# A transformer layer on one core: row maxima as a stream of their own, w_out scaled within its split, another order in the first chunk

## The chip, the cores and the metric

The kernel runs on one core of one Trainium2 chip. The metric is the device time of one execution in microseconds, from the kernel's start to its end. The core has a matmul engine (PE, with PEld for its weight loads), a vector engine (DVE), an activation engine (ACT), a general engine (POOL) and an engine that issues transfers (SP); each works through its own list of instructions in order, and they wait for one another by semaphores.

## What is computed

One layer over 2,048 positions of width 1,024 in float32:

```
xn = rms_norm(x, mix_norm_g);  h = xn @ w_in
q, k, v, f_logit, z = split(h)                  # 8 heads of 64; z is 2 x 512
c = cumsum(log_sigmoid(f_logit + b_f))
s[t, u] = q_t . k_u / 8 + c[t] - c[u],  u <= t
attn = softmax(s) @ v
zu, zv = split(gelu(z));  zv = layer_norm(zv)
sgu = zu * (w_s (masked, 128 x 128 per group) @ zv + b_s)
merged = concat(rms_norm(attn), rms_norm(sgu))  # times out_norm_g
x = x + merged @ w_out
xn = rms_norm(x, ffn_norm_g);  gate, up = split(xn @ w_gate_up)
x = x + (silu(gate) * up) @ w_down
out = rms_norm(x, final_norm_g)
```

## The kernel before

Matmul operands are kept as two parts, a high one (`hi_of`, a rounding cast, on ACT) and the rest (`lo_of`, value minus high part, on DVE or POOL), and each product is three matmuls: high by high, high by low, low by high. The source emits instructions in an order that serves as priority; a scheduler then fixes each engine's list at build time by its own estimate of when operands are ready, so an engine's list need not follow the source. What a list holds is then kept to on the chip: an instruction that waits holds up all behind it.

**Projection (stage 1).** The positions go in four chunks of 512. For each, x is loaded transposed, scaled and split (`Chunk.halves`), the split is stored to memory as XS for later use (`Chunk.keep`, two stores of 512 KB for each of four parts), row squares of the untransposed x give the norm r1 (`Chunk.square`), and r1 is turned to a row by transposes on PE (`Chunk.row`, L270). Weights come in four pieces each through `weight` or `whole`: a load from POOL's queue into one of two raw buffers, a cast on ACT, a subtraction on DVE. In the first chunk v is projected first (`v_part`, into four PSUM banks of the tag "mm"); `v_close` scales and splits the four results (ACT L428, DVE L429), and the gate matmuls L482 take the first bank that comes free. Then come four groups of 24 matmuls for q and four for k (L509). After each group `between` advances three generators: the forget gates of this chunk (`forget_rows`: an ACT and DVE chain up to lf, then transposes and products on PE from L311 on, the result stored as AUG), the preparation of the next chunk (`Chunk.steps`) and the early row maxima.

**Row maxima.** The softmax needs the maximum of each query row over its keys. `one_max` is one matmul (L337, 128 queries by up to 512 keys, into one of two PSUM buffers) and one DVE reduction (L339, or with the causal mask L342). For a head h and a query chunk j there are 4(j+1). `max_split` and `max_rows` bring the result to memory (md), from where it joins the query tile A as two more rows. `early_max(j)` does heads 0 to 7 of chunks 0 and 1 and heads 0 to 4 of chunk 2 within stage 1, with query and key tiles (A, D) of its own. What is left, chunk 3 of all heads and chunk 2 of heads 5 to 7, is done in `prep`.

**Attention (stage 2).** The 32 units (h, j) run head by head; a unit has 4(j+1) steps, 320 in all. A step is `qk` (two matmuls L624 and L625, a mask L627 on the diagonal, exp on ACT L629, the split of the result, Ph on ACT and Pl on DVE) and, one step later, `pv_of` (L640 to L642). At a unit's first step `prep` is started for the unit two ahead (AHEAD): it loads keys, values and queries and, where the maxima are still missing, spreads them over this one unit's steps. Between the steps runs `gates`: the z projection (`z_proj`, L672, 256 k steps), GELU, norm and `z_mix`, spread by a count over the steps up to ZEND = 293. Before the loop starts, w_s is loaded, masked and split, and the norm's constants are loaded (L933 to L942). The split of w_u, z's first weight, stands at the end of stage 1.

**w_out.** From step 276 on, as soon as z's k steps are all issued, `out_weights` takes one slice of 128 x 512 a step, 16 in all: POOL multiplies it by out_norm_g (`gain`, L799), ACT casts it, POOL subtracts. At step 300 the output stage begins (`out_tiles`), then the FFN, whose matmuls L1296 fill the span from some 1,250 us on.

## Time and profile before

| | us |
|---|---|
| three runs | 2510.0, 2509.7, 2504.14 |
| median | 2509.7 |
| the profiled execution | 2512.58 |
| its span, first to last instruction | 2510.8 |
| PE busy in it | 2437.3 |

All rows below are from that one profiled execution; times in rows count from the start of its span. The profile says of each instruction when it ran, how long the engine had been idle before it, and what released it. A matmul's end is modelled, so the time from one start to the next says more than the duration.

### The profile page before, as it was taken

Reading aid. Unit: us, or ns where it says so; the run is one execution under the profiler, and the core shown is the slowest. Engines: PE = TensorE matmul, PEld = TensorE weight load, DVE = VectorE, ACT = ScalarE, POOL = GpSimd, SP = SyncE. Lnnn points to the kernel's source line nnn. Section 1 sums busy time; section 2 is a strip of 40 time slices with the busy share of each in tenths; the row PEclk is TensorE's granted clock in tenths of the full one; section 3 lists DMA queues with packets and bytes.
Section 4 is the critical chain, followed back from the end, with each engine's and each line's share of the span. In section 5 each row is a group of like instructions: output and inputs, shape, how many; then the busy total and the mean of one; then the engine's idle time right before and its main releaser. Section 6 shows DMA issues by size and latency. Waiting matters only on the chain. (4 is left out here: it accounts for less than half of the span.)

```text
span 2510.8 us, 31035 instructions
## 1 busy us (share of the span) xinstructions
PE 2437.3 (97%) x10857; PEld 1949.1 (78%) x10857; DVE 1562.2 (62%) x2537; ACT 1054.5 (42%) x1787; POOL 555.6 (22%) x442
## 2 busy tenths in 40 slices
PE   7899999999999989999999999999999999999998
PEld 5677777787777776877788888878888877888876
DVE  4457485555456666455755555775555587586887
ACT  4312236667777666333423333433232342232333
POOL 1000000000000024122223323233232234454441
PEclk9999999999999988999999999999999999999999
DMA  9766574334433336665422232342322335455454
GB/s 307 259 223 207 162 210 131 93 99 108 112 95 96 89 88 171 187 207 174 159 84 85 84 93 68 93 142 76 93 68 84 93 109 193 168 180 187 134 189 150
DMA packets 351646, 348.25 MB, mean 139 GB/s; under 512 B 54428, under 2 KB 275092, under 8 KB 350466
## 3 DMA queue, kind: packets, MB, share of 16 engines
q1 hardware_dynamic: 349186, 337.88, 43.5%
q0 software_dynamic: 2304, 8.39, 1.1%
q8 instruction: 86, 1.41, 0.2%
q14 instruction: 70, 0.57, 0.1%
HBM read 229.47 MB, written 116.72 MB: 138 GB/s over the span
## 5 line engine op out<-in xcount | busy, mean ns | idle before, releaser
L102 ACT CAST wh<-raw 128x512 fp32r<-128x512 f32 (+2 forms) x500 | 309.3, 624 | 803.0 <-PE pp L1296 648.3
L107 DVE TENSOR_TENSOR wl<-raw,wh 128x512 fp32r<-128x512 f32 (+2 forms) x500 | 371.6, 752 | 116.5 <-ACT wh L102 115.2
L107 DVE TENSOR_TENSOR Pl<-Pt,Ph 128x512 fp32r<-128x512 f32 (+1 forms) x320 | 201.3, 635 | 198.0 <-ACT Ph L102 190.2
L1027 POOL TENSOR_TENSOR raw<-raw 128x512 f32<-128x512 f32 (+1 forms) x124 | 166.3, 1342 | 542.3 <-DMA raw<-in_w_gu_dram 374.1
L629 ACT ACTIVATE Pt<-st 128x512 f32<-128x512 f32 (+1 forms) x320 | 168.4, 532 | 157.0 <-PE st L625 83.3
L672 PE MATMUL z<-wh,xz 128*128 128x512 f32 x512 | 201.6, 403 | 0.0
L102 ACT CAST Ph<-Pt 128x512 fp32r<-128x512 f32 (+1 forms) x320 | 176.2, 556 | 13.5 <-DVE Pl L107 2.4
L1027 DVE TENSOR_TENSOR raw<-raw,raw 128x512 f32<-128x512 f32 (+1 forms) x112 | 133.4, 1192 | 73.1 <-POOL raw L1027 69.2
L339 DVE TENSOR_REDUCE mx<-mx_ps 128x1 f32<-128x512 f32 x192 | 127.9, 685 | 29.2 <-PE mx_ps L337 28.1
L642 PE MATMUL pv<-Pl,V 128*128 128x512 f32 (+1 forms) x320 | 121.9, 381 | 11.2 <-DVE Pl L107 11.2
L337 PE MATMUL mx_ps<-D,A 72*128 72x512 f32 (+5 forms) x320 | 121.8, 402 | 11.3 <-DVE mx L339 5.9
L624 PE MATMUL st<-A,D 74*128 74x512 f32 (+1 forms) x320 | 121.5, 380 | 1.8 <-ACT Pt L629 1.7
L640 PE MATMUL pv<-Ph,V 128*128 128x512 f32 (+1 forms) x320 | 122.7, 383 | 0.4 <-ACT Ph L102 0.3
L625 PE MATMUL st<-B,C 128*128 128x512 f32 (+1 forms) x320 | 119.7, 374 | 0.0
L641 PE MATMUL pv<-Ph,V 128*64 128x512 f32 (+1 forms) x320 | 117.0, 366 | 0.0
L672 PEld LDWEIGHTS z<-wh,xz 128*128 128x128 f32 x512 | 96.7, 189 | 18.9
L1296 PE MATMUL pp<-R2h,wh 128*128 128x512 f32 x264 | 105.2, 398 | 4.9 <-ACT u L1085 4.9
L1296 PE MATMUL pp<-R3h,wl 128*128 128x512 f32 x264 | 104.3, 395 | 2.6 <-DVE wl L107 2.6
L1296 PE MATMUL pp<-R2h,wl 128*128 128x512 f32 x264 | 105.0, 398 | 0.2 <-DVE wl L107 0.2
L1296 PE MATMUL pp<-R1h,wl 128*128 128x512 f32 x264 | 104.4, 395 | 0.7 <-DVE wl L107 0.7
L1296 PE MATMUL pp<-R2l,wh 128*128 128x512 f32 x264 | 104.5, 396 | 0.0
L1296 PE MATMUL pp<-R5h,wh 128*128 128x512 f32 x264 | 104.4, 395 | 0.0
(338 smaller groups left out, 6203.0 us busy)
## 6 DMA issues: line engine op xcount, KB each, us to landing
raw<-in_w_gu_dram SPq DMA_DIRECT2D x88, 512.0 KB
HD<-hT SPq DMA_DIRECT2D x44, 512.0 KB
xz<-XS SPq DMA_DIRECT2D x32, 512.0 KB
XA<-xa SPq DMA_DIRECT2D x27, 512.0 KB
xa<-XA SPq DMA_DIRECT2D x24, 512.0 KB
raw<-HD SPq DMA_DIRECT2D x24, 512.0 KB
xb<-XA SPq DMA_DIRECT2D x24, 512.0 KB
XA<-xb SPq DMA_DIRECT2D x21, 512.0 KB
```

Of the source, the lines that this page charges most:

```text
L102: nc.scalar.copy(o, i)
L107: eng.tensor_tensor(o, i, f(h), ALU.subtract)
L337: nc.tensor.matmul(pm[:, 0:n], lhs, Dt[0 : lhs.shape[0], 0:n], start=True, stop=True)
L339: nc.vector.tensor_reduce(mx[:, a, s : s + 1], pm, AX.X, ALU.max)
L624: nc.tensor.matmul(st[:, off:], Dt[:, b * P : (b + 1) * P], A[:, off:], start=True, stop=False)
L625: nc.tensor.matmul(st[:, off:], C[:, b * P : (b + 1) * P], B[:, off:], start=False, stop=kb < 4 * j)
L629: nc.scalar.activation(Pt[:, off:], st[:, off:], AF.Exp)
L640: nc.tensor.matmul(pv[:, off:], V[:, 0:P], Ph[:, off:], start=kb == 0, stop=False)
L642: nc.tensor.matmul(pv[:, off:], V[:, 0:P], Pl[:, off:], start=False, stop=kb == 4 * j + 3)
L672: nc.tensor.matmul(pz, xz[:, a, k, :], w[b][:, k, :], start=n == 0, stop=n == 3 * KT - 1)
L1027: (nc.vector if e == "v" else nc.gpsimd).tensor_tensor(o, a, b, op)
L1296: nc.tensor.matmul(pm, a[:, k, :], b[:, k, :], start=on is None and k == 0 and e == 0, stop=k == it.kh - 1 and e == 2, skip_group_check=n ...
```

## The change

- `forget_rows` gives way three times in place of once before its transposes, for chunks 0 and 1.
- `early_max` becomes `max_stream`, which takes a list of units, pools and buffer counts. Stage 1 calls it for the same units as before. Stage 2 calls it once for all that are left, with two query and two key tiles of its own in a new pool, loaded one key tile ahead; it is advanced by a count, 166 turns over LEND = 276 steps with a lead of 12. `prep` has no maxima any more. `max_due` runs the stream on where a unit that starts within three steps still lacks them.
- w_q's pieces 2 and 3 are loaded and split after `v_close` rather than before the v projection.
- The XS stores of chunk 0 move from its own q groups to those of chunk 1.
- The split of w_u moves from the end of stage 1 into z's first six k steps; w_s and the constants of the norm (`z_consts`) are loaded at z's third k step and split at its thirteenth.
- In `out_weights` ACT scales by out_norm_g as it casts, and one DVE operation scales and subtracts; POOL's two operations go, and so does one empty step.

```diff
+LEND = 276
...
-        yield
+        for _ in range(3 if j < 2 else 1):
+            yield
...
-    def early_max(j):
-        jobs = [(h, s) for h in range(HE[j]) for s in range(j + 1)]
+    def max_stream(units, pl, ps, pp, nd, ahead):
+
+        jobs = [(h, j, s) for h, j in units for s in range(j + 1)]
...
                 if s == 0:
-                    A = As[h] = T(p1, [66, CH], F32R, "A")
+                    A = As[h, j] = T(pl, [66, CH], F32R, "A", bufs=2)
...
-                Dt = Ds[n] = T(p1, [66, CH], F32R, "D", bufs=ND)
+                Dt = Ds[n] = T(pl, [66, CH], F32R, "D", bufs=nd)
                 ldr(Dt[0:64], KH[pr][s][o : o + DH])
                 ldr(Dt[64:66].rearrange("r (b t) -> r b t", t=P), aug_rows(h, s, slice(2 * j, 2 * j + 2)))
-        late = None
-        PF = j + 1
-        for n in range(PF):
+        def turn():
+            max_rows(pp, T(ps, [P, 4, P], F32, "mx_ps" if ps is ps2_[0] else "tp", **kw), *late)
+        late, kw = None, {"bufs": NMX} if ps is ps2_[0] else {}
+        for n in range(ahead):
             get(n)
-        for n, (h, s) in enumerate(jobs):
-            get(n + PF)
+        for n, (h, j, s) in enumerate(jobs):
+            get(n + ahead)
             if s == 0:
-                mx = T(p1, [P, 4, 4], F32, "mx")
+                mx = T(pp, [P, 4, 4], F32, "mx")
             for a in range(4):
-                one_max(ps1, p1, a, j, s, As[h][:, a * P : (a + 1) * P], Ds[n], mx)
+                one_max(ps, pp, a, j, s, As[h, j][:, a * P : (a + 1) * P], Ds[n], mx)
                 yield
                 if a == 2 and late is not None:
-                    max_rows(p1, T(ps1, [P, 4, P], F32, "tp"), *late)
+                    turn()
                     late = None
             if s == j:
-                late = (h, j, max_split(p1, j, mx))
-        yield
-        max_rows(p1, T(ps1, [P, 4, P], F32, "tp"), *late)
+                late = (h, j, max_split(pp, j, mx))
+        yield
+        turn()
...
-    wq = whole(wgt, w_in[:, 0:512], "w")
+    wq, get_q, halves_q = weight(wgt, w_in[:, 0:512], "w")
+    for i in range(2):
+        get_q(i)
+        halves_q(i)
     load_mats()
...
     nxt.row()
     for tt in range(4):
         v_close(pms[tt], nxt, tt)
+    for i in range(2, 4):
+        get_q(i)
+        halves_q(i)
     wk = whole(wgt, w_in[:, 512:1024], "w")
...
+                if c == 1 and which == 0:
+                    first.keep(pr)
                 qh = T(p1, [P, CH], F32R, "qh")
                 ql = T(p1, [P, CH], F32R, "ql")
                 if c == 0:
-                    if which == 0:
-                        xc.keep(pr)
...
-        early = early_max(c) if c < NCH - 1 else iter(())
-    for i in range(4):
-        if i > 1:
-            get_u(i)
-        halves_u(i)
-
+        early = max_stream([(h, c) for h in range(HE[c])], p1, ps1, p1, ND, c + 1) if c < NCH - 1 else iter(())
     st1.close()
...
+    p2m = pool(stz, "p2m", bufs=2)
...
-        if (h, j) not in MD:
-            mx = T(p2, [P, 4, 4], F32, "mx")
-            for a in range(4):
-                for s in range(j + 1):
-                    one_max(ps2, p2, a, j, s, A[0:72, a * P : (a + 1) * P], kd[h, s][1], mx)
-                    yield
-            mh = max_split(p2, j, mx)
-            yield
-            yield
-            max_rows(p2, T(ps2, [P, 4, P], F32, "mx_ps", bufs=NMX), h, j, mh)
-        ldr(A[72:74], MD[h, j].rearrange("(r b) t -> r (b t)", r=2))
-        yield
+        if (h, j) in MD:
+            ldr(A[72:74], MD[h, j].rearrange("(r b) t -> r (b t)", r=2))
+        else:
+            due.append((h, j))
+
+    def max_due(u):
+
+        if u in due:
+            due.remove(u)
+            while u not in MD:
+                next(lm)
+            ldr(ab[u][0][72:74], MD[u].rearrange("(r b) t -> r (b t)", r=2))
...
+    ZC = {}
+
+    def z_consts():
+        wsr = T(p2z, [P, 8, P], F32, "zr", bufs=2)
+        ld(wsr, w_st.rearrange("g j i -> j g i"))
+        bsc = T(p2z, [P, 8], F32, "bsc", bufs=1)
+        ld(bsc, b_st)
+        lngb = T(p2z, [P, 512], F32, "lngb", bufs=1)
+        ld(lngb, ln_g.rearrange("(o n) -> o n", o=1).broadcast_to([P, 512]))
+        lnbb = T(p2z, [P, 512], F32, "lnbb", bufs=1)
+        ld(lnbb, ln_b.rearrange("(o n) -> o n", o=1).broadcast_to([P, 512]))
+        ZC.update(bsc=bsc, lngb=lngb, lnbb=lnbb)
+        yield
+        nc.vector.memset(wsr[64:128, :, 0:64], 0.0)
+        hi_of(nc.scalar, wst_h, wsr)
+        lo_of(nc.vector, wst_l, wsr, wst_h)
+        yield
...
+                    if i == cc == 0 and (g, k) in ((1, 2), (0, 4)):
+                        next(zc)
+                    if i == cc == 0 and g and k in (0, 1, 4, 5):
+                        n_u = (0, 1, 4, 5).index(k)
+                        halves_u(n_u)
+                        if n_u < 2:
+                            get_u(n_u + 2)
                     yield
...
-        def gain(e):
-            if e < 2 * len(jobs):
-                n, i = divmod(e, 2)
-                kh, fh, pr = jobs[n]
-                k = kh * 4 + pr * 2 + i
-                r = raw[n][:, i, :]
-                nc.gpsimd.tensor_tensor(r, r, E["onc"][:, k : k + 1].broadcast_to([P, CH]), ALU.mult)
-
         get(0)
         get(1)
         yield
-        yield
-        gain(0)
         yield
         for e in range(2 * len(jobs)):
             n, i = divmod(e, 2)
             kh, fh, pr = jobs[n]
-            gain(e + 1)
+            g = E["onc"][:, kh * 4 + pr * 2 + i : kh * 4 + pr * 2 + i + 1]
             if e % 4 == 0:
                 W[kh, fh] = resident({(0, 0): 0, (1, 0): 2, (0, 1): 5, (1, 1): 6}[kh, fh])
             h_, l_ = (w[:, pr * 2 + i, :] for w in W[kh, fh])
-            hi_of(nc.scalar, h_, raw[n][:, i, :])
-            lo_of(nc.gpsimd, l_, raw[n][:, i, :], h_)
+            nc.scalar.activation(h_, raw[n][:, i, :], AF.Copy, scale=g)
+            nc.vector.scalar_tensor_tensor(l_, raw[n][:, i, :], g, f(h_), ALU.mult, ALU.subtract)
             if i:
                 get(n + 2)
...
-            for _ in prep(*u, ab):
-                pass
-    wsr = T(p2z, [P, 8, P], F32, "zr", bufs=2)
-    ld(wsr, w_st.rearrange("g j i -> j g i"))
-    nc.vector.memset(wsr[64:128, :, 0:64], 0.0)
-    hi_of(nc.scalar, wst_h, wsr)
-    lo_of(nc.vector, wst_l, wsr, wst_h)
...
+            prep(*u, ab)
+    zc = z_consts()
...
-    pg, p_total, p_done = iter(()), 0, 0
+    rest = [u for u in units if u[1] == NCH - 1 or u[0] >= HE[u[1]]]
+    lm, l_total, l_done = max_stream(rest, p2m, ps2, p2, 2, 1), sum(4 * j + 4 for _, j in rest) + 2, 0
     for n in range(len(steps) + DEPTH):
         if n < len(steps):
             h, j, kb = steps[n]
-            if kb == 0:
-                for _ in pg:
-                    pass
-                ui = units.index((h, j)) + AHEAD
-                if ui < len(units):
-                    pg, p_done = prep(*units[ui], ab), 0
-                    p_total = 4 * (units[ui][1] + 1) + 3 if units[ui] not in MD else 1
-                else:
-                    pg, p_total = iter(()), 0
+            if kb == 0 and units.index((h, j)) + AHEAD < len(units):
+                prep(*units[units.index((h, j)) + AHEAD], ab)
+            max_due(steps[min(n + 3, len(steps) - 1)][0:2])
             qk(h, j, kb)
-            while p_done < p_total * (kb + 1) / (4 * j + 4):
-                next(pg, None)
-                p_done += 1
+            while l_done < l_total * (n + 12) / LEND:
+                next(lm, None)
+                l_done += 1
             while z_done < z_total * n / ZEND:
                 next(zg, None)
                 z_done += 1
```

(Uses of `lngb`, `lnbb` and `bsc` in z become `ZC[...]`; `first` is the chunk object of chunk 0.)

## Rows read from the trace of the kernel before

**Rows 1.** Page, part 1: busy us, share of the span, instructions.

```profile
PE 2437.3 (97%) x10857; PEld 1949.1 (78%) x10857; DVE 1562.2 (62%) x2537; ACT 1054.5 (42%) x1787; POOL 555.6 (22%) x442
```

**Rows 2.** Stretches: length, busy us (instructions) per engine, PE clock, DMA share, GB/s.

```profile
0.00:106.00 106.00, 85.53 (x352) 65.24 (x353) 50.61 (x80) 45.33 (x67) 10.96 (x18) 0.92 0.89 308
106.00:210.00 104.00, 100.75 (x447) 78.94 (x446) 53.98 (x169) 29.77 (x49) 1.01 (x1) 0.98 0.60 197
315.00:362.00 47.00, 46.24 (x205) 36.36 (x203) 43.51 (x110) 9.34 (x13) 3.79 (x7) 1.00 0.65 199
362.00:378.00 16.00, 11.26 (x44) 8.56 (x45) 6.84 (x11) 10.96 (x22) 0.00 (x0) 0.79 0.91 249
400.00:900.00 500.00, 493.78 (x2422) 395.40 (x2422) 283.00 (x590) 348.98 (x639) 16.00 (x17) 1.00 0.37 100
916.00:976.00 60.00, 49.50 (x187) 37.23 (x186) 49.32 (x92) 39.91 (x78) 35.99 (x30) 0.74 0.39 118
966.00:976.00 10.00, 10.00 (x49) 7.81 (x48) 5.75 (x11) 9.47 (x20) 0.00 (x0) 0.93 0.61 182
1500.00:1525.00 25.00, 25.00 (x110) 20.22 (x109) 16.26 (x22) 7.71 (x13) 9.64 (x7) 1.00 0.28 81
```

**Rows 3.** Timeline, first chunk: start, us, engine, line, what [idle before <-releaser].

```profile
32.26 1.04 ACT L102 CAST wh<-raw 128x1024 fp32r<-128x1024 f32 x1 [1.54 <-DMA raw<-in_w_in_dram]
...
36.92 1.84 ACT L428 ACTIVATE xh<-mm,r 128x512 fp32r<-128x512 f32 x3
...
38.29 2.71 DVE L429 SCALAR_TENSOR_TENSOR xh<-mm,r,xh 128x512 fp32r<-128x512 f32 x4
...
39.08 0.65 PE L482 MATMUL mm<-xh,wf 128*40 128x512 f32 x1 [6.31 <-DVE xh L429]
```

**Rows 4.** Timeline, first chunk, later.

```profile
31.45 0.42 SPq L98 DMA_DIRECT2D XS<-xh  x1
...
53.84 0.34 SPq L98 DMA_DIRECT2D XS<-xl  x1
...
54.30 0.58 SPq L255 DMA_DIRECT2D xt<-in_x_dram  x1
...
62.98 1.06 ACT L260 ACTIVATE jk<-xt 128x1024 bf16<-128x1024 f32 x1 [3.17 <-DMA xt<-in_x_dram]
...
64.42 1.04 POOL L264 TENSOR_TENSOR r<-r1a,mhalf 128x4 f32<-128x4 f32 x1 [4.97 <-DVE r1a L263]
...
69.49 0.47 PE L311 MATMUL tp<-ident,v 128*128 128x128 f32 x1 [9.17 <-DVE v L308]
```

**Rows 5.** Timeline, seam between projection and attention.

```profile
370.58 0.48 DVE L934 MEMSET zr<- 64x512 f32 x1 [4.59 <-DMA zr<-in_w_st_dram]
...
371.10 1.04 ACT L102 CAST wsth<-zr 128x1024 fp32r<-128x1024 f32 x1 [3.03 <-DVE zr L934]
...
371.84 0.79 PE L642 MATMUL pv<-Pl,V 128*128 128x512 f32 x1 [3.49 <-DVE Pl L107]
...
372.18 1.23 DVE L107 TENSOR_TENSOR wstl<-zr,wsth 128x1024 fp32r<-128x1024 f32 x1 [0.39 <-ACT wsth L102]
...
373.29 0.63 PE L640 MATMUL pv<-Ph,V 128*128 128x512 f32 x1
...
373.72 0.63 PE L641 MATMUL pv<-Ph,V 128*64 128x512 f32 x1
```

**Rows 6.** Groups, 916 to 976: xcount, busy us, mean ns, idle before.

```profile
L337 PE MATMUL mx_ps<-D,A 72*128 72x512 f32 (+3 forms) x28 | 14.0, 520 | 4.1 <-DVE mx L339 2.1 <-DVE mx L342 1.9
...
L339 DVE TENSOR_REDUCE mx<-mx_ps 128x1 f32<-128x512 f32 x20 | 13.2, 681 | 4.8 <-PE mx_ps L337 4.6
...
L102 ACT CAST R6h<-xa 128x512 fp32r<-128x512 f32 x4 | 2.5, 620 | 3.2 <-POOL xa L799 3.2
```

**Rows 7.** Timeline of DVE before and within POOL's work.

```profile
912.59 0.42 DVE L107 TENSOR_TENSOR Pl<-Pt,Ph 128x256 fp32r<-128x256 f32 x1 [0.97 <-ACT Ph L102]
...
930.16 2.33 DVE L107 TENSOR_TENSOR Pl<-Pt,Ph 128x256 fp32r<-128x256 f32 x2
```

More of the change, by code (lines that the diff above doesn't have):

```diff
@@ L430, in v_close @@
         ldr(VD[xc.c][:, tt * P : (tt + 1) * P, :].rearrange("h p d -> p h d"), v)
-    nxt = Chunk(0)
+    nxt = first = Chunk(0)
     still = T(p1, [P, CH], F32R, "D", bufs=ND)
@@ L689, in z_proj @@
             zv = zr[:, cc, 512:1024]
-            nc.vector.scalar_tensor_tensor(zv, zv, mv[:, cc, 0:1], lngb, ALU.subtract, ALU.mult)
-            nc.vector.scalar_tensor_tensor(zv, zv, rv[:, cc : cc + 1], lnbb, ALU.mult, ALU.add)
+            nc.vector.scalar_tensor_tensor(zv, zv, mv[:, cc, 0:1], ZC["lngb"], ALU.subtract, ALU.mult)
+            nc.vector.scalar_tensor_tensor(zv, zv, rv[:, cc : cc + 1], ZC["lnbb"], ALU.mult, ALU.add)
             zv8 = zv.rearrange("p (g d) -> p g d", g=8)
@@ L709, in z_mix @@
                 nc.vector.scalar_tensor_tensor(sg[:, :, g * DH : (g + 1) * DH],
-                                               px[:, g4, :].rearrange("p (c d) -> p c d", c=2), bsc[:, g : g + 1],
+                                               px[:, g4, :].rearrange("p (c d) -> p c d", c=2), ZC["bsc"][:, g : g + 1],
                                                zr[:, :, g * DH : (g + 1) * DH], ALU.add, ALU.mult)
@@ L921, in out_tiles @@
                 E["half"] = fh
-    ab = {}
+    ab, due = {}, []
     AHEAD = 2
@@ L929, in trunk @@
         for u in units[:AHEAD]:
-            for _ in prep(*u, ab):
-                pass
-    wsr = T(p2z, [P, 8, P], F32, "zr", bufs=2)
-    ld(wsr, w_st.rearrange("g j i -> j g i"))
-    nc.vector.memset(wsr[64:128, :, 0:64], 0.0)
-    hi_of(nc.scalar, wst_h, wsr)
-    lo_of(nc.vector, wst_l, wsr, wst_h)
-    bsc = T(p2z, [P, 8], F32, "bsc", bufs=1)
-    ld(bsc, b_st)
-    lngb = T(p2z, [P, 512], F32, "lngb", bufs=1)
-    ld(lngb, ln_g.rearrange("(o n) -> o n", o=1).broadcast_to([P, 512]))
-    lnbb = T(p2z, [P, 512], F32, "lnbb", bufs=1)
-    ld(lnbb, ln_b.rearrange("(o n) -> o n", o=1).broadcast_to([P, 512]))
+            prep(*u, ab)
+    zc = z_consts()
     zg = gates()
```

2 lines of the change are left out of this document (1 added, 1 removed).

## The prediction

> **What bounds the kernel now.** I read the page's busy shares first: the matmul engine (PE) is busy 97% of the span [rows 1], so a part of this change can only pay where PE idles or runs at the lower clock. The table of stretches shows where that is. In the FFN, as from 1500 to 1525, PE has its full clock and no gaps; the full rate there is 110 matmuls in 25 us, 0.227 us each. Three stretches fall short of it [rows 2]: the first chunk (0 to 106 us: busy 85.5, clock 0.92), the seam between projection and attention (362 to 378: 11.3 of 16, clock 0.79), and 916 to 976, where the z projection has run out and w_out is split (49.5 of 60, clock 0.74). The long middle (400 to 900) lacks 6.2 us in 500.
>
> Then the timeline of each weak stretch, for what ends its waits.
>
> First chunk: the gate matmul L482 starts at 39.08 after 6.31 us of waiting for a PSUM bank that v_close empties; ACT does v_close from 36.92 on, behind casts of w_q pieces such as the one at 32.26, which waited for its load [rows 3]. Later the transpose L311 waits 9.17 us, until 69.49, for the forget-gate chain [rows 4].
>
> Seam: DVE stands 4.59 us in front of a memset that needs w_st; the cast of w_st waits for it on ACT and holds up the attention's cast behind it; PE waits 3.49 us until 371.84, then runs at 0.43 us a matmul (373.29 to 373.72), the lower clock level of 1.2 GHz [rows 5].
>
> Late stretch: DVE has 49.3 us of work in 60 and POOL 36.0 [rows 2]; 28 of the row maxima fall here, 20 of them plain reductions of 0.68 us each [rows 6]. And DVE is slowed while POOL works: Pl at 128x256 takes 0.42 us before POOL is busy, 2.33 us for two at 930 [rows 7].
>
> **The change part by part.** The sum is made against the profiled execution, 2512.58 us (span 2510.8 and 1.8 around it).
>
> *A. First chunk.* Two of four w_q pieces, with their loads, casts and subtractions, come behind v_close. The casts hold ACT from 32.26 to 36.92 [rows 3], so L482 can come up to 4.7 us earlier. The two added steps before the gate's transposes put L311 two projection groups (48 matmuls, 10.9 us at 0.227) later for chunks 0 and 1, more than the 9.17 us it waits. But what is late next stands right behind L311 in PE's order: the transposes of r (L270) for chunk 1. r is ready when POOL's power ends, 64.42 + 1.04 = 65.46; it hangs on a row square at 62.98, which waits 3.17 us for an x tile whose load was issued only at 54.30 [rows 4]. So without L311's wait PE goes on at 65.46 at the earliest unless r moves: 4.0 us gained, and L482's 4.7 us only lengthen that wait. r does move, because the eight 512 KB stores of the split x (XS) leave this chunk: four are issued from 31.45 to 53.84, ahead of that load [rows 4]. 2 MB at the stretch's 308 GB/s with the queues 89% busy [rows 2] is 6.8 us. I take half, since the load also waits for its buffer: r at 62.1, so 69.5 - 62.1 = 7.4 us gained. Ends: 19.5 if both waits and the slow matmuls behind them (some ten at 0.43 for 0.227, 2 us each) all go; -1 if w_k's casts, now behind w_q's late ones, hold the squares back.
>
> *B. XS in chunk 1.* The eight stores pass on SP in front of q's stores; the loads for the early maxima, the gate rows and the next x queue behind them. 4 MB at 308 GB/s is 13.6 us of transfer; the stretch has its queues 60% busy over 104 us [rows 2], so the free 40% covers it. Where an early maximum's key tile comes late, PE waits: it lacks 3.25 us there now. Taken: -1; ends 0 and -4.
>
> *C. Seam.* The w_st memset and casts move 12 z steps on, the loads of constants leave the front of SP's queue: 3.49 us plus ten slow matmuls (2.0) come back, 5.5. w_u's split moves here: four subtractions at 1.23 us like that at 372.18 [rows 5], and the first step issues eight maxima at once (166 turns x 12/276 = 7.2), 5.4 us by 0.68: 10.3 us for a DVE with 9.2 free in 362 to 378 [rows 2]. In exchange DVE is relieved at 315 to 362, where it is busy 43.5 of 47 [rows 2]. I set 2 against it: +3.5; ends +6 and -4 (a w_u cast that waits on ACT for its late third piece holds the exponentials, as the w_st cast does now).
>
> *D. Maxima as a stream.* All 164 maxima that are left, with their masks and transposes, run at 0.6 a step from the first to step 264 instead of in bursts of 12 to 16 within 4 to 8 steps. Matmul and reduction are the same. New are 41 key tiles and 11 query tiles, 104 issues on SP and 6.9 MB, hidden under queues 37% busy [rows 2]. PE lacks 6.2 us in the middle; +1.5, ends +5 and -1. The 28 maxima of the late stretch move into this saturated PE: 28 x 0.227 = 6.4 us, counted in E.
>
> *E. w_out.* 32 POOL operations go (POOL's 36.0 us in the stretch, bar two small powers). ACT's 16 casts of 0.62 us [rows 6] become scaled copies; v_close's scaled copies take 1.84 for three, 0.61 [rows 3], so I allow 0.1 each, 1.6 in all. DVE gets 16 fused operations at 0.68 (v_close's four take 2.71 [rows 3]), 10.9 us, and loses 28 maxima: 20 x 0.68 and eight of up to that, some 18. DVE ends near 42 at most, ACT at 39.9 + 1.6 = 41.5 [rows 2]; the 159 matmuls left need at most 36 at the full rate. ACT then sets the pace. In 966 to 976, attention without maxima and POOL, ACT is busy 9.47 of 10 at clock 0.93 [rows 2]: 41.5/0.947 = 43.8 us for the 60. 60 - 43.8 - 6.4 = +9.8. The other end is the second rival, -6.4. Taken +8, near the row that looks most like the new stretch.
>
> On this part the Trainium skill ("TensorE: Matmul & The Clock Gate", section "A second HAM failure mode: psum-queue depth-cycling") says that PE, pausing often between groups of matmuls, can swing between its two clock levels and lose throughput though each wait is short. That speaks against E: an ACT-paced PE pauses in every step. By it E is the -6.4 of the second rival, and the sum 5.0 in place of 19.4; the 0.74 of the present stretch fits it, the 0.93 of 966 to 976 less.
>
> **Sum:** 7.4 - 1 + 3.5 + 1.5 + 8 = 19.4 us. 2512.6 - 19.4 = 2493.2 for such an execution; the median of the runs is 2.9 lower, so 2509.7 - 19.4 = **2490.3**.
>
> **Rivals.**
> *First chunk opens fully.* If r and the gate chain both come before PE needs them, A is 19.5: gain 31.5, 2478. For it: queues near 90% busy lose 4 MB. Against: the x load is released by an earlier square, not by bandwidth alone.
> *The late stretch stays 60 us.* PE stays at half clock: 159 matmuls at up to 0.43 are up to 68 us, more than ACT's 41.5, and the 28 maxima cost 6.4 elsewhere. Gain 19.4 - 8 - 6.4 = 5.0, 2504.7.
> *The stalls only change their name, or the order does not change.* ACT's order is not the source's: the copy of r's row is written before the four v_close copies, yet three of them run first. If the w_q casts still run first and r keeps its time, A is 4.0; if w_u's split eats the seam, C is 0: gain 12.5, 2497; with A at -1 too, 7.5, 2502.
> *Slower.* A key tile's load waits on SP for PE's maxima two jobs back (two buffers), and the loads of the unit two ahead, z's inputs and the results' stores queue behind it. A job is four maxima, 6.6 steps; a step is about 1.8 us (2422 matmuls in 500 us, 8.7 a step), so 12 us against a lead of at least 12 steps, 22 us. That hides it. It decides once the 32 units' loads come over 0.6 us late on average (19.4/32); at 1 us each the cost is 32, gain -12.6, 2522.
>
> **How the numbers follow.** Chances: forecast 0.48 (own range 2483 to 2499), open chunk 0.15, late stretch unchanged 0.12, renamed stalls 0.17, slower 0.08. A measurement of this kernel tells 0.3%, 7.5 us, from no change, so faster means below 2502.2 and slower above 2517. Forecast, open chunk and most of the third are faster: 0.79; the second and the rest: 0.13 within; slower 0.08. Range 2472 to 2508: it leaves out the far half of the open chunk and the slower case, and takes in the ends of A and E.
>
> **What would show it.** L482 before 36 us and no wait of L311; a wait of L270 that ends near 62. At the seam no DVE wait for w_st. No L337 after step 264; in the late stretch POOL almost empty, DVE's Pl at 0.4 to 0.7 us throughout, ACT over 90% busy and some 45 us in place of 60. Wrong would be: the same stretch at clock 0.7 and as long as now; a first chunk whose next gate matmuls start no earlier; key loads with SP waits of 10 us and units that start late.

## The result, and the profile after

| | before | after |
|---|---|---|
| median of 4 runs each, us | 2508.01 | 2481.5 |
| range | 2504.14 to 2510.0 | 2479.89 to 2487.48 |
| the profiled execution | 2512.58 | 2479.89 |

The ratio is 0.9901 with a 95% interval of 0.9879 to 0.9922: 26.5 us faster by the medians, 32.7 by the two profiled executions, of which the one before is slower than any of its four runs and the one after is the fastest of its four. The forecast was 2490.3 in 2472 to 2508. The direction and the range hold; the gain was forecast at 19.4 us.

Line numbers have moved: the gate matmul is L493 now, the lf transpose L313, r's transposes L271, the maxima L339, L341 and L344, Pl's subtraction L108, and w_out's scaled cast and fused subtraction L836 and L837.

First the page's part 1 of the kernel after (busy us, share of the span, instructions), for [rows 1]:

```profile
PE 2418.2 (98%) x10857; PEld 1939.2 (78%) x10857; DVE 1568.0 (63%) x2553; ACT 1055.4 (43%) x1787; POOL 520.5 (21%) x410
```

Then stretches of the kernel after, for [rows 2]: chunk 0 up to chunk 1's gate matmuls, chunk 1, the first 20 attention steps, the long middle, steps 279 to 302 and 302 to 319. Columns as in [rows 2].

```profile
0.00:99.14 99.14, 81.17 (x331) 62.50 (x331) 48.52 (x77) 44.08 (x65) 10.98 (x18) 0.93 0.88 304
99.14:178.02 78.88, 78.26 (x354) 61.15 (x352) 40.30 (x128) 21.62 (x35) 1.01 (x1) 1.00 0.71 240
357.89:395.80 37.91, 37.17 (x175) 29.61 (x176) 26.98 (x51) 24.20 (x46) 0.00 (x0) 1.00 0.70 189
400.00:900.00 500.00, 497.04 (x2466) 402.43 (x2464) 299.78 (x631) 350.67 (x643) 13.37 (x14) 1.00 0.42 114
901.52:946.86 45.34, 36.19 (x162) 24.77 (x161) 34.09 (x67) 40.22 (x80) 3.65 (x5) 0.92 0.53 160
946.86:991.51 44.65, 44.47 (x208) 35.66 (x209) 26.13 (x43) 25.94 (x48) 7.20 (x10) 1.00 0.68 189
```

The reader is to see two things: the late stretch is 45.3 us with POOL at 3.65 and ACT at 40.22 of it, and the middle issues 44 matmuls more in the same 500 us than before.

Where the time went is read from PE's timeline, at the starts of the same matmuls in both traces (a step is counted by its first pv matmul):

| from | to | before | after | gain |
|---|---|---|---|---|
| start of the span | chunk 1's gate matmuls | 101.10 | 99.14 | 2.0 |
| there | chunk 2's gate matmuls | 83.24 | 78.88 | 4.4 |
| there | step 0 | 179.73 | 179.87 | -0.1 |
| step 0 | step 20 | 46.20 | 37.91 | 8.3 |
| step 20 | step 279 | 505.59 | 505.72 | -0.1 |
| step 279 | step 302 | 60.40 | 45.34 | 15.1 |
| step 302 | step 319 | 47.26 | 44.65 | 2.6 |

These add to 32.0 of the 32.7. Each is read from one trace of either kernel, and traces in which the lists are the same differ too. Eight kernels with one list up to chunk 1's gate matmuls (the kernel after and seven of the experiments) start these at 97.5 to 100.7 us; eight with this seam, stream and w_out (the kernel after and seven experiments on the first two chunks) take 37.8 to 39.7 us for steps 0 to 20 and 45.3 to 47.8 us for steps 279 to 302. So the first row's 2.0 us is hardly clear of repeats, and the 8.3 and the 15.1 stand at the upper end of theirs.

That the middle gains nothing in length hides a gain: 28 maxima more are done up to step 279. If from each stretch the matmuls' own time at the full rate is taken off (0.232 us for one of 512 columns and less for fewer, the start-to-start times where PE has no gap), what is left from step 20 to 264 is 31.3 us before and 23.1 after. The two figures hang on what the narrow matmuls are priced at; their difference of some 8 us hardly does.

The first chunk of the kernel after, its timeline (columns as in [rows 3]):

```profile
31.18 1.02 SPq L256 DMA_DIRECT2D xt<-in_x_dram  x2
...
32.06 1.04 ACT L103 CAST wh<-raw 128x1024 fp32r<-128x1024 f32 x1 [1.66 <-DMA raw<-in_w_in_dram]
...
34.70 1.04 ACT L103 CAST wh<-raw 128x1024 fp32r<-128x1024 f32 x1 [1.59 <-DMA raw<-in_w_in_dram]
35.65 1.84 ACT L433 ACTIVATE xh<-mm,r 128x512 fp32r<-128x512 f32 x3
...
36.60 0.34 SPq L99 DMA_DIRECT2D XS<-xh  x1
...
37.00 0.41 SPq L99 DMA_DIRECT2D XS<-xl  x1
...
38.12 0.65 PE L493 MATMUL mm<-xh,wf 128*40 128x512 f32 x1 [5.67 <-DVE xh L434]
...
46.55 3.44 SPq L99 DMA_DIRECT2D XS<-xh  x1
...
50.59 1.81 SPq L256 DMA_DIRECT2D xt<-in_x_dram  x2
...
62.12 1.04 POOL L265 TENSOR_TENSOR r<-r1a,mhalf 128x4 f32<-128x4 f32 x1 [4.09 <-DVE r1a L264]
...
63.22 1.12 PE L271 MATMUL tp<-ident,r 128*128 128x128 f32 x4 [7.70 <-POOL r L265]
```

Against [rows 3] and [rows 4]: both late w_q casts still run ahead of v_close, although the source has them behind it; the gate matmul has gained 0.96 us. The wait of L311 is gone, and one of 7.70 us for r stands in its place, 6.3 us earlier. Nor have the XS stores all left the chunk, although the source has all eight in chunk 1: three are still issued there before r, where the kernel before issues four [rows 4], and five come in chunk 1. What has changed is their place on SP: the first two loads of x stand ahead of them, at 31.18 in place of 37.56, and the fourth is issued at 51.84 in place of 54.30.

DVE's costliest group in the late stretch of the kernel after, and ACT's and DVE's new operations on w_out (columns as in [rows 6]):

```profile
L108 DVE TENSOR_TENSOR Pl<-Pt,Ph 128x512 fp32r<-128x512 f32 (+3 forms) x24 | 13.8, 586 | 3.3 <-ACT Ph L103 3.3
L837 DVE SCALAR_TENSOR_TENSOR R6l<-xa,onc,R6h 128x512 fp32r<-128x512 f32 x4 | 3.0, 752 | 1.4 <-ACT R6h L836 1.4
L836 ACT ACTIVATE R6h<-xa,onc 128x512 fp32r<-128x512 f32 x4 | 2.9, 726 | 0.3 <-DMA xa<-in_w_out_dram 0.3
L741 DVE SCALAR_TENSOR_TENSOR sg<-z,bsc,zr 128x128 f32<-128x128 f32 x8 | 2.2, 328 | 0.0
```

No maxima are left there. The pair of Pl that took 2.33 us in [rows 7] is one of 256 columns and one of 128; these widths take 0.43 and 0.28 us now (timeline):

```profile
925.64 0.43 DVE L108 TENSOR_TENSOR Pl<-Pt,Ph 128x256 fp32r<-128x256 f32 x1
...
928.11 0.28 DVE L108 TENSOR_TENSOR Pl<-Pt,Ph 128x128 fp32r<-128x128 f32 x1
```

### The profile page after: what moved, and what is told of

Same layout as the page of the kernel before. It is cut to its first block, busy times and chain, and to the rows that moved or that the text cites. A ratio compares the mean times of both kernels' runs of the same rounds, so it can differ in the third digit from the quotient of the medians.

```text
span 2477.8 us, 31118 instructions
## 1 busy us (share of the span) xinstructions
PE 2418.2 (98%) x10857; PEld 1939.2 (78%) x10857; DVE 1568.0 (63%) x2553; ACT 1055.4 (43%) x1787; POOL 520.5 (21%) x410
## 5 line engine op out<-in xcount | busy, mean ns | idle before, releaser
L108 DVE TENSOR_TENSOR wl<-raw,wh 128x512 fp32r<-128x512 f32 (+2 forms) x500 | 377.6, 763 | 114.2 <-ACT wh L103 113.7
L108 DVE TENSOR_TENSOR Pl<-Pt,Ph 128x512 fp32r<-128x512 f32 (+1 forms) x320 | 193.0, 610 | 158.4 <-ACT Ph L103 157.0
L341 DVE TENSOR_REDUCE mx<-mx_ps 128x1 f32<-128x512 f32 x192 | 130.9, 687 | 39.4 <-PE mx_ps L339 36.4
L339 PE MATMUL mx_ps<-D,A 66*128 66x512 f32 (+2 forms) x320 | 119.6, 385 | 4.2 <-DVE mx L341 2.8
```

The costliest lines, as they stand in the source:

```text
L108: eng.tensor_tensor(o, i, f(h), ALU.subtract)
L339: nc.tensor.matmul(pm[:, 0:n], lhs, Dt[0 : lhs.shape[0], 0:n], start=True, stop=True)
L341: nc.vector.tensor_reduce(mx[:, a, s : s + 1], pm, AX.X, ALU.max)
```

## The experiments

All are edits of the kernel after, with the whole computation kept. Medians stand beside their ratio to the kernel before, run on the same chips; "excess" is time against the kernel after's 2481.5, which was run at another time. The kernel before's own medians beside these runs are 2506.5 to 2508.2, so an excess is uncertain by some 2 us, and the ratio is the safer figure.

### The late stretch: w_out's form and the stream, each undone and both

**w_out as before, stream kept.**

```diff
-            nc.scalar.activation(h_, raw[n][:, i, :], AF.Copy, scale=g)
-            nc.vector.scalar_tensor_tensor(l_, raw[n][:, i, :], g, f(h_), ALU.mult, ALU.subtract)
+            gain(e + 1)
...
+            hi_of(nc.scalar, h_, raw[n][:, i, :])
+            lo_of(nc.gpsimd, l_, raw[n][:, i, :], h_)
```

> The changed kernel with w_out's split as before: POOL scales each slice, ACT casts, POOL subtracts, one empty step more. The maxima stay a stream. In the changed kernel the 23 steps from step 279 to step 302 take 45.4 us, before 60.4. Theory 1, POOL's work and what it does to DVE sets the pace of that stretch: it takes 52 to 60 us and the run is 7 to 15 us over the changed kernel, 2488 to 2496. Rival, the 28 maxima that have left the stretch filled DVE, and w_out's form matters little: the stretch takes 44 to 48 us and the run is within 3 us of the changed kernel's 2481.5.

2490.25 us, ratio 0.9937 (0.9924 to 0.9949): excess 8.8.

**Maxima in prep as before, w_out new.**

```diff
-    p2m = pool(stz, "p2m", bufs=2)
...
+        if (h, j) not in MD:
+            mx = T(p2, [P, 4, 4], F32, "mx")
+            for a in range(4):
+                for s in range(j + 1):
+                    one_max(ps2, p2, a, j, s, A[0:72, a * P : (a + 1) * P], kd[h, s][1], mx)
+                    yield
...
-            while l_done < l_total * (n + 12) / LEND:
-                next(lm, None)
+            while p_done < p_total * (kb + 1) / (4 * j + 4):
+                next(pg, None)
```

> The changed kernel with the maxima of stage 2 in prep again, in bursts within one unit, with the unit's own tiles; w_out new. Steps 20 to 264 have 23.1 us over the plain issue time in the changed kernel and 31.3 before, although 27 maxima (some 6 us) have moved into them. Theory 1, the stream is worth about 8 us in the middle and costs its 6 us there, and w_out's split carries the late gain: the middle is 2 us longer than in the changed kernel, the stretch 279 to 302 some 50 to 52 us (6 us for 28 maxima), the run 2488 to 2492. Rival, the maxima alone had filled the late stretch: it takes 57 us or more again, the run 2495 to 2500.

2500.64 us, ratio 0.9979 (0.997 to 0.9987): excess 19.1.

**Both of these edits.**

> The changed kernel with both undone: maxima in prep, w_out on POOL. What is left is the first chunks' order, the XS stores and the seam. By the milestones of the two traces these are worth 2.0 to 7 us up to the first step and 5.5 at the seam, 12 us together: 2496, with the stretch 279 to 302 at 60 us. If gain and loss of the two parts simply add, this run's excess over the changed kernel is the sum of the excesses of the two runs with one undone; if either alone frees the stretch, it is far more than the sum; if both are needed, each run alone shows the whole.

2502.95 us, ratio 0.9987 (0.9978 to 0.9996): excess 21.5.

Steps 279 to 302 in the three, as stretches (columns as in [rows 2]): w_out old, then maxima in prep, then both. They are three views, one for each kernel.

```profile
901.77:955.04 53.27, 40.77 (x159) 29.96 (x158) 34.46 (x49) 39.44 (x79) 38.91 (x31) 0.74 0.42 128
```

```profile
908.28:962.79 54.51, 44.26 (x189) 33.09 (x188) 48.66 (x109) 41.14 (x78) 1.76 (x2) 0.87 0.37 111
```

```profile
907.00:967.01 60.01, 48.53 (x190) 36.22 (x188) 49.35 (x92) 39.93 (x78) 35.91 (x30) 0.77 0.41 119
```

From 60.0 us the new w_out alone takes 5.5 us (to 54.5), the stream alone 6.7 (to 53.3), both 14.7 (to 45.3). The first expectation's theory 1 is met (53.3 us, 8.8 over). The second's is not: its price, 19.1 us, lies at the upper end of its rival's, though the stretch stayed under the rival's 57. The trace says where the rest is: the first 20 steps take 43.2 us in place of 37.9, steps 302 to 319 take 51.3 in place of 44.7, and from step 20 to 264 31.7 us are over the plain issue time in place of 23.1. The third expectation's sum, 2496, is missed: it counted the seam's gain as kept, but with the maxima in prep the first 20 steps take 43.5 us even with w_s and w_u moved. By medians neither part is worth a fixed sum: w_out's form is worth 2.3 us without the stream (2502.95 - 2500.64) and 8.8 with it; the stream 12.7 with the old w_out and 19.1 with the new. That the two prices do not add is shown; why is not. Both ease DVE, but with w_out old DVE is busy only 34.5 of 53.3 us.

What POOL does to DVE is seen in DVE's groups of the same stretch. First w_out old with the stream:

```profile
L108 DVE TENSOR_TENSOR Pl<-Pt,Ph 128x512 fp32r<-128x512 f32 (+3 forms) x23 | 23.2, 1027 | 14.1 <-ACT Ph L103 14.0
L741 DVE SCALAR_TENSOR_TENSOR sg<-z,bsc,zr 128x128 f32<-128x128 f32 x8 | 2.3, 338 | 0.4 <-PE z L736 0.4
```

Then both undone, and last the maxima in prep with POOL idle:

```profile
L108 DVE TENSOR_TENSOR Pl<-Pt,Ph 128x512 fp32r<-128x512 f32 (+3 forms) x23 | 20.0, 891 | 2.6 <-ACT Ph L103 2.6
L341 DVE TENSOR_REDUCE mx<-mx_ps 128x1 f32<-128x512 f32 x20 | 13.2, 682 | 4.9 <-PE mx_ps L339 4.9
```

```profile
L108 DVE TENSOR_TENSOR Pl<-Pt,Ph 128x512 fp32r<-128x512 f32 (+3 forms) x24 | 13.8, 583 | 0.6 <-ACT Ph L103 0.6
L341 DVE TENSOR_REDUCE mx<-mx_ps 128x1 f32<-128x512 f32 x20 | 13.3, 684 | 2.0 <-PE mx_ps L339 2.0
```

The mean Pl takes 0.583 and 0.586 us where POOL is idle, 0.891 and 1.027 where POOL works. The reductions out of PSUM do not care (0.682 against 0.684). (The means mix widths; at 512 columns alone Pl takes 0.68 to 0.69 us where POOL is idle, 0.86 and 1.18 where it works.) With w_out old, DVE is not full, but each step's chain from exp to the last pv matmul is longer, and PE's clock falls to 0.74.

POOL holds the stretch up in a second way. In ACT's list the casts of w_out wait for POOL's multiplication, and the next exponential stands behind them. With w_out old and the stream, ACT stands 10.1 us in all before these casts, and 8.2 us with both undone. PE's two longest waits with w_out old, 6.7 us together, are for an exponential: one behind the GELU, and this one (timeline of w_out old with the stream):

```profile
923.55 0.62 ACT L103 CAST R2h<-xa 128x512 fp32r<-128x512 f32 x1 [2.56 <-POOL xa L831]
...
925.07 0.59 ACT L636 ACTIVATE Pt<-st 128x512 f32<-128x512 f32 x1
...
925.72 0.58 PE L631 MATMUL st<-A,D 74*128 74x256 f32 x1 [2.55 <-ACT Pt L636]
```

PE's waits for Pl itself are 2.3 us there. How much of the 8.8 us is Pl's slower subtraction and how much ACT's wait for POOL no run separates.

**The stream with its own tiles, but advanced in the old bursts.**

```diff
-            while l_done < l_total * (n + 12) / LEND:
+            while l_done < min(plan[n], l_total):
```

> The changed kernel, its stream with own key and query tiles kept, but advanced as before: a unit's 12 to 16 maxima within the steps of the unit two ahead of it, so that 28 fall behind step 279 again. Theory 1, it is the spreading that pays (no bursts, none in the late stretch), not the tiles: the run equals the one with maxima in prep, 2499 to 2502, steps 20 to 264 have some 31 us over the plain issue time, the stretch 279 to 302 takes 54 us. Rival, the tiles of its own pay (a maximum need not wait for the unit's key tile and query tile): steps 20 to 264 stay near 23 us over, the run is 2484 to 2492.

2496.2 us, ratio 0.9953 (0.994 to 0.9965): excess 14.7, near theory 1 but 3 to 6 us under it. Steps 20 to 264 have 30.9 us over the plain issue time (23.1 spread evenly, 31.7 in prep), the stretch 279 to 302 takes 50.0, with 22 maxima in it and not 28. So spreading makes most of the stream's 19.1 us, 14.7 by the medians and 13 by the ratios; the rest, 4 to 7, is left for the tiles of its own. The largest part of the excess, 9.0 us, falls in steps 302 to 319 (53.6 in place of 44.7), where no maximum is left in either kernel: PE waits there for Pl and for sums and weights of the output stage. Why the bursts push this work there is open.

### The seam

**w_u's split back to the end of stage 1, w_s and the constants back before the first step.**

```diff
+    for i in range(4):
+        if i > 1:
+            get_u(i)
+        halves_u(i)
...
-    zc = z_consts()
+    for _ in z_consts():
+        pass
```

> The changed kernel with the seam as before: w_u's last two pieces loaded and all four split at the end of stage 1, w_s and the norm's constants loaded and split before the first step. The first 20 steps have 2.0 us over the plain issue time in the changed kernel, 7.5 before. Theory 1, the wait for w_s and the slow matmuls behind it are the whole price of the seam: 5 to 6 us come back, 2486 to 2488. Rival, the seam's gain came from the maxima that no longer have to be made for the first units at once: the first 20 steps stay under 4 us over, and the run is within 2 us of 2481.5.

2484.84 us, ratio 0.9913 (0.99 to 0.9927): excess 3.3, less than theory 1 had, and its interval and the kernel after's overlap. The first 20 steps take 43.4 us in place of 37.9 and have 7.2 us over the plain issue time in place of 2.0; against the 37.8 to 39.7 of the eight traces named above that is 3.7 to 5.6 us, which the median bears out at its lower end. Its timeline at the seam has the wait of [rows 5] again, at the same instructions:

```profile
365.48 0.48 DVE L685 MEMSET zr<- 64x512 f32 x1 [4.92 <-DMA zr<-in_w_st_dram]
...
366.74 0.80 PE L654 MATMUL pv<-Pl,V 128*128 128x512 f32 x1 [3.81 <-DVE Pl L108]
```

In the kernel after, the view of PE's waits for these 20 steps has one line (us in total, times, longest):

```profile
PE mx_ps L339 <- DMA D<-AUG: 0.7, 1, 0.7
```

### The first two chunks

**The forget gates give way once, in both chunks**, and **once in chunk 1 only.**

```diff
-        for _ in range(3 if j < 2 else 1):
+        for _ in range(1):
```

> The changed kernel with the forget gates giving way once, as before, in chunks 0 and 1. The lf transpose stands in front of the first chunk's third group of q again and waits for its chain, which ends near 68. Theory 1, the two added steps gain what the milestones show, 2 us up to chunk 1's gate matmuls and 4.4 us in chunk 1: the run is 2486 to 2489 and chunk 2's gate matmuls start 6 us later than in the changed kernel (184 in place of 178). Rival, the gain comes from the w_q pieces and XS alone: within 2 us of 2481.5, gate matmuls of chunk 2 within 1.5 us of 178.0.

2478.82 us, ratio 0.9886 (0.9873 to 0.99): 2.7 under the kernel after. The rival's milestone is met, its time missed by 0.7 us: chunk 2's gate matmuls start at 177.10. L313 waits 7.08 us, until 67.69, and L271 for chunk 1 no longer does; the wait changes its name and nearly keeps its size.

```diff
-        for _ in range(3 if j < 2 else 1):
+        for _ in range(3 if j < 1 else 1):
```

> The changed kernel with the two added steps in chunk 0 alone. Chunk 1 is 78.9 us from gate matmuls to gate matmuls in the changed kernel and 83.2 before. If the added steps of chunk 1 make that difference, chunk 1 takes 82 to 84 us here and the run is 4 us longer, 2485 to 2486. Rival, chunk 1 gained because the first chunk hands it its early maxima and gates in another order: it stays at 79 us and the run within 1.5 us of 2481.5.

2482.6 us, ratio 0.9913 (0.9897 to 0.9929); chunk 1 takes 78.72 us. The rival's numbers again.

**All of w_q ahead of v.**

```diff
-    wq, get_q, halves_q = weight(wgt, w_in[:, 0:512], "w")
-    for i in range(2):
-        get_q(i)
-        halves_q(i)
+    wq = whole(wgt, w_in[:, 0:512], "w")
...
-    for i in range(2, 4):
-        get_q(i)
-        halves_q(i)
```

> The changed kernel with all of w_q ahead of v in the source again. The lists that the scheduler makes of it are, instruction for instruction and on all five engines, those of the changed kernel (only buffer numbers differ), so that this part of the change should be worth nothing: 2481.5 within 2 us, and first gate matmuls at 38.1. The run is at the same time a repeat of the changed kernel on other days' chips and shows what a difference of medians is worth. Rival, buffers differ and with them the places in memory that a tile gets: more than 4 us off.

2480.0 us, ratio 0.9897 (0.9882 to 0.9913), gate matmuls at 37.96. The w_q part of the change is worth nothing, because the scheduler makes the same lists with it and without it. As a repeat of the kernel after it also says that medians differ by 1.5 us for nothing.

**XS of chunk 0 in chunk 0 again.**

```diff
-                if c == 1 and which == 0:
-                    first.keep(pr)
...
                 if c == 0:
+                    if which == 0:
+                        xc.keep(pr)
```

> The changed kernel with the XS stores of chunk 0 in chunk 0 again. Of the 2 us by which chunk 1's gate matmuls came earlier and the 4.4 us that chunk 1 itself became shorter, neither the forget gates' steps nor w_q's pieces have a share. Theory 1, XS has both: chunk 1's gate matmuls start 2 us or more later than at 99.1, chunk 1 takes 81 to 83 us in place of 78.9, the run is 2485 to 2490. Rival, chunk 1 is shorter by the early maxima, whose function has two query tiles and another order now: chunk 1 stays at 79 us and the run within 3 us of 2481.5.

2483.4 us, ratio 0.9905 (0.9889 to 0.9921). Half and half: chunk 1's gate matmuls start at 103.08, as theory 1 had it, but chunk 1 takes 79.63 and the run is within 3 us, as the rival had it. Its timeline shows why the gate matmuls are late: XS stores stand on SP ahead of the loads of x again. The first two loads are issued at 37.75 in place of 31.18, the third at 52.96 in place of 50.59, and PE gets r 3.65 us later. In all fourteen traces r is done 10.0 to 11.9 us after the fourth load of x for chunk 1 is issued, and that issue is at 54.3 and 55.6 where XS stands as before, at 50.1 to 52.7 where it is moved.

```profile
38.61 0.43 SPq L99 DMA_DIRECT2D XS<-xh  x1
52.96 0.42 SPq L256 DMA_DIRECT2D xt<-in_x_dram  x1
...
66.87 1.12 PE L271 MATMUL tp<-ident,r 128*128 128x128 f32 x4 [10.01 <-POOL r L265]
```

With both undone (gates and XS), the lists of all five engines up to the first attention step are, but for buffer numbers, those of the kernel before (as built; it was not run); so the trace of the kernel before is the fourth corner of this table of PE's timeline:

| | gates and XS as before | gates later | XS later | both (after) |
|---|---|---|---|---|
| the wait in chunk 0 | L311 9.17 | L271 10.01 | L313 7.08 | L271 7.70 |
| chunk 1's gate matmuls | 101.10 | 103.08 | 98.90 | 99.14 |
| chunk 2's gate matmuls | 184.34 | 182.71 | 177.10 | 178.02 |
| chunk 1 | 83.24 | 79.63 | 78.20 | 78.88 |

Up to chunk 2's gate matmuls XS alone brings all of the 6.3 us, which seven traces with the kernel after's list there (177.2 to 179.8) bear out; the whole run's median, with XS back, is only 1.9 us longer, not clear of the 1.5 that a repeat shows. The gates' later place seems to cost 2 us in chunk 0 where XS is not moved, within the spread of repeats, and is worth nothing where it is. Chunk 1 gets shorter by either. In the kernel before, DVE waits there for a late tile of x, the scaling and splitting of x then stand ahead of a maximum, and PE waits for it; the clock from 142 to 152 is 0.83 (timeline of the kernel before, chunk 1):

```profile
140.97 1.23 DVE L241 TENSOR_TENSOR xt<-xt,rb 128x1024 f32<-128x1024 f32 x1 [2.07 <-DMA xt<-in_x_t_dram]
...
147.29 0.38 PE L337 MATMUL mx_ps<-D,A 66*128 66x256 f32 x1 [1.74 <-DVE mx L342]
```

Of the three waits for L342 there, 3.2 us in all, one of 0.55 is left after.

**v_close really ahead.** The late casts of w_q, and the constant's cast on DVE, first write one element of v_close's last result into their targets, so that no list can have them before it.

```diff
+        nc.vector.tensor_copy(crr[0:1, 0:1], f(last[0:1, 0, DH : DH + 1]))
         nc.vector.tensor_copy(crr, cr)
...
         get_q(i)
+        nc.scalar.copy(wq[0][0:1, 2 * i, 0:1], f(last[0:1, 0, 0:1]))
         halves_q(i)
```

> The changed kernel with v_close really ahead of w_q's late casts on ACT, and of the constant's cast on DVE: each of these first takes one element of v_close's last result into its target, which it then overwrites. Theory 1, as the prediction had it for this step: the first gate matmuls come 2.5 to 4 us earlier (34 to 35.6 in place of 38.1), but the wait for r only grows by as much, and chunk 1's gate matmuls and the run stay within 2 us of the changed kernel (99.1 and 2481.5). Rival, w_q's later pieces then make PE wait in the first q group: 2 us later or more.

2481.66 us, ratio 0.9898 (0.9882 to 0.9914). Theory 1, with a first gate matmul still earlier than it said (timeline):

```profile
33.48 0.43 PE L496 MATMUL mm<-xh,wf 128*40 128x512 f32 x1 [0.85 <-DVE xh L435]
62.28 1.11 PE L272 MATMUL tp<-ident,r 128*128 128x128 f32 x4 [13.70 <-POOL r L266]
```

The gate matmul gains 4.64 us, the wait for r takes 6.0 us more, and chunk 1's gate matmuls start 0.75 us earlier, inside the spread of repeats.

**r's transposes for chunk 1 six turns later** (v_close as in the kernel after).

```diff
+            for _ in range(6 if self.c == 1 else 0):
+                yield
             self.row()
```

> The changed kernel with six more turns before the transposes of r for chunk 1, so that they stand behind the first 96 q and k matmuls of the first chunk and no longer behind 49. In the changed kernel PE waits 7.7 us there, until 63.2. Theory 1, that wait is the whole rest of the first chunk's loss: it goes, chunk 1's gate matmuls start at 92 to 94 in place of 99.1, the run is 2474 to 2477. Rival, the split of x for chunk 1, which needs r's row, is then late: PE waits in front of chunk 1's gate matmuls, which start at 97 or later, and the run is 2480 to 2483.

2474.07 us, ratio 0.9871 (0.9856 to 0.9886): 7.4 under the kernel after by medians, 7.6 by the profiled executions, the fastest of all. Theory 1 is met in time; chunk 1's gate matmuls start at 90.66, earlier still than it said. The wait for r is gone, and in its place PE's timeline has

```profile
67.23 0.33 PE L315 MATMUL tp<-ident,v 128*128 128x128 f32 x1 [0.65 <-DVE v L311]
```

**Both of the last two, with r behind 120 matmuls.**

> The kernel with r's transposes late (2474 us) with the same edit, and with r's transposes behind 120 matmuls in place of 96. Theory 1, r was all that kept the earlier start from counting: chunk 1's gate matmuls start at 86 to 88 in place of 90.7 and the run is 2470 to 2472. Rival, the split of chunk 1's x ended at 90.4 there, with transfers at a share of 0.9 to 1.0 from 30 us on, and becomes the wait that takes over: the gate matmuls of chunk 1 wait and start at 89 or later, the run is 2473 to 2476.

2476.15 us, ratio 0.9879 (0.9862 to 0.9896): no gain over the kernel with r late alone; the rival's numbers, but not its cause. The start that comes 4.6 us earlier is waited away again at neither of the places named: chunk 1's gate matmuls start at 92.12, and what PE waits for is the forget gates' chain. It ends at 66.7 here, and at 67.2 and 67.6 in the two other kernels where the lf transpose stands early enough to wait for it (r late, gates once), although the gate matmuls start 4.6 us earlier here. One reason stands in ACT's list: the row squares of chunk 1's x come ahead of the chain there, and the first of the last two waits 9.19 us for its tile, so the late loads of x hold the gates' chain as they hold r.

```profile
57.45 1.06 ACT L262 ACTIVATE jk<-xt 128x1024 bf16<-128x1024 f32 x1 [9.19 <-DMA xt<-in_x_dram]
...
66.78 0.48 PE L316 MATMUL tp<-ident,v 128*128 128x128 f32 x1 [5.62 <-DVE v L312]
```

## Why the prediction was right, and where it was off

The sum came out at 19.4 us for 32.7 measured by the profiled executions and 26.5 by the medians, by terms that missed in both directions. That A and B together came out at 6.4 us, forecast and measured, is luck: one was 5.4 too high, the other 5.4 too low. By the table the missing 12.6 us are the seam (8.3 for 3.5), the middle (-0.1 for D's 1.5 less the 6.4 of the maxima moved into it), the late stretch (15.1 for 14.4) and steps 302 to 319 (2.6, not forecast).

**A, the first chunk, 7.4 forecast, 2.0 measured (0.4 to 3.6 against the eight traces).** The step that failed is "So without L311's wait PE goes on at 65.46 at the earliest ... r at 62.1, so 69.5 - 62.1 = 7.4 us gained". r was done at 63.2, near enough, but the gain was read from the times of two waits as if both transposes stood at one place in PE's order. In the kernel after, r's stand behind 49 of the chunk's q matmuls, the lf transpose before stood behind 68. PE leaves the wait 6.3 us earlier with some 19 matmuls more to do, 4.3 us at 0.227. Standing later, behind 96, r's transposes cost nothing and give 7.6 us (the kernel with r late). That L482's earlier start "only lengthen[s] that wait" was right, and is shown by the kernel with v_close ahead. "L482 before 36 us" did not come, since the third rival's case is true of w_q: the order does not change. XS was rightly named as what moves r: 3.65 us between the kernels with and without it, 3.4 forecast. But that the sizes meet is luck, for the stated reason failed: the forecast took half the transfer time of four stores that leave, and three of the four are still issued ahead of the last load of x. What the traces show is order on SP: the fourth load is issued 3.7 us earlier (51.84 for 55.56), and r follows it.

**B, chunk 1, -1 forecast, +4.4 measured.** The step that failed took XS as mere load on the queues there, eight stores where five come. It reckoned with maxima that wait for key tiles; the waits before were for DVE, behind a late x tile, and that tile comes earlier when chunk 0 ends earlier or in another order. Which of the reordered instructions does it in each corner of the table is not settled.

**C, the seam, 3.5 forecast, 5.2 to 5.5 by the trace**, 3.7 against its slowest repeat, 3.3 by the median. The 2 us set against it for w_u and the burst of eight maxima did not show in the kernel after's trace, whose 20 steps have one wait of 0.7 us. The rest of the 8.3 us there goes with the maxima: in prep, the first 20 steps take 43.2.

**D, the stream, 1.5 forecast for the middle.** Undersized: 8.2 us less over the plain issue time between steps 20 and 264. The forecast looked at "6.2 us" that PE lacked in busy time, where the gaps are shorter than the modelled matmul ends let one see; the start-to-start times, with the prices above, have 31.3. The slower rival is out: the middle is no longer than before, and the longest wait of an SP issue in it fell from 11.2 us to 9.3.

**E, w_out with the 28 maxima, 8 + 6.4 forecast for the late stretch, 15.1 measured.** The size holds, and the mechanism as far as the trace tells: 45.3 us with ACT busy 40.2 (89%), the fullest engine, for 43.8 forecast at 94.7%; no run gives ACT less to do. ACT is idle 5.1 us where the forecast left 2.3, and 3.0 of them are for PE. The largest single pause is the GELU's: ACT's two table loads and the GELU take 1.28 + 1.91 + 1.28 us, PE waits 4.28 us for the exponential behind them with no maxima left to fill it, and ACT then waits 1.40 us for PE, which runs at a low clock by then (timeline of the kernel after):

```profile
901.08 1.28 ACT L711 ACT_TABLE_LOAD   x1
902.37 1.91 ACT L711 ACTIVATE zr<-zr 128x2048 f32<-128x2048 f32 x1
904.30 1.28 ACT L636 ACT_TABLE_LOAD   x1
...
906.24 0.58 PE L631 MATMUL st<-A,D 74*128 74x256 f32 x1 [4.28 <-ACT Pt L636]
...
914.63 0.60 ACT L636 ACTIVATE Pt<-st 128x512 f32<-128x512 f32 x1 [1.40 <-PE st L632]
```

ACT's scaled cast is 0.726 us, 0.1 over the plain one of [rows 6], as allowed. What the forecast did not see is that it takes both parts, w_out's and the stream's; it put the 8 down to w_out, which alone gives 5.5 of that stretch and 2.3 of the whole. The second rival, 60 us at half clock, is out: the granted clock is 0.92.

The Trainium skill ("TensorE: Matmul & The Clock Gate", section "A second HAM failure mode: psum-queue depth-cycling") was cited against E. Its swinging clock is seen here where POOL works (0.74 and 0.77), less with the maxima in prep (0.87), and in the kernel after only behind the GELU's wait, as the next section shows.

Another page bears on E: the Trainium skill ("SBUF — State Buffer", section "SBUF: two separate sides") says that among the engines only the port pair that VectorE and GpSimd share brings contention, and that a VectorE operation with two SBUF inputs can be blocked by a GpSimd one that reads SBUF. By that rule Pl, with two SBUF inputs, should stretch under POOL and operations fed from PSUM should not; the trace agrees, with Pl at 0.89 to 1.03 us against 0.58, and L341 and L741 unchanged (0.68, and 0.338 against 0.328).

## What to carry to other kernels

Where two waits stand in one engine's list, ask not only when each ends but how much work of that engine stands behind each: removing the later one is worth the difference only if the earlier one stands no earlier in the list. Read the built list, not the source, before an edit of order is given a price: of this change one part (w_q) left every list as it was, and another (XS) moved five stores of eight. Small reductions that compete with a latency chain are cheap when spread one at a time over a long stretch and dear in bursts, and how dear depends on what else holds the same engine, so such edits are priced together. And trace one list more than once: a stage of one and the same list differed by some 3 us here, more than some of the gains read from single traces.

## What the runs showed of the hardware

After its wait of 4.28 us PE ran 5 us at a granted clock of 0.52 (near the level of 1.2 GHz) and the next 5 at 0.79, and then stayed at 1.00 (2.4 GHz) for 35 us although it was busy only 3.84 to 4.34 us of some of the 5 us stretches (stretches of the kernel after):

```profile
906.00:911.00 5.00, 4.23 (x13) 3.39 (x14) 4.41 (x9) 4.67 (x12) 1.06 (x1) 0.52 0.26 65
911.00:916.00 5.00, 5.00 (x32) 4.69 (x31) 4.72 (x12) 3.57 (x8) 0.00 (x0) 0.79 0.51 150
...
926.00:931.00 5.00, 3.84 (x21) 2.23 (x19) 2.81 (x8) 4.15 (x11) 0.70 (x1) 1.00 0.55 171
```

With w_out on POOL, PE is busy 2.19 of 5 us between 922 and 927 (with the wait of 2.55 us for an exponential that stands behind POOL's multiplication), and the clock is 0.63 there and 0.50 in the 10 us behind it:

```profile
922.00:927.00 5.00, 2.19 (x8) 1.23 (x6) 2.31 (x6) 3.04 (x6) 5.00 (x6) 0.63 0.35 108
927.00:937.00 10.00, 8.78 (x30) 6.53 (x29) 7.93 (x9) 7.27 (x19) 9.51 (x8) 0.50 0.32 109
```

PE is busy 8.78 us of these 10. By an estimate from a matmul's 0.43 us at the low level and 0.227 at the full one, some 4 us of that is the lower clock, so the pause can cost more than its own length; how much of it reached the run's time no run shows.
